# The down projection of the second feed-forward block: 16 of 22 contraction tiles by seven block products

## The chip, the cores and the metric

One Trainium2 chip, one of its cores. The metric is the device time of one execution in microseconds; a kernel's time is the median of its runs. A profile is one further execution with the hardware profiler, and the times of single instructions come from it. Engines are called TensorE (PE in the profile), VectorE (DVE), ScalarE (ACT), GpSimd (POOL) and SyncE (SP, which only issues transfers).

## The reference

One layer of a streaming encoder on x of 512 tokens by 1024 features, all in float32:

```
h = x + 0.5 * post1(SwiGLU_1(pre1(x)))          # SwiGLU: (silu(x @ w1) * (x @ w3)) @ w2
u = pre_mix(h)                                   # each pre/post: RMS norm with a gain
q, k, v, x_rnn, x_gate = split(u @ w_in)
y_a = (rg_lru(conv4(x_rnn)) * gelu(x_gate)) @ w_lru_out
y_b = sliding_window_attention(q, k, v) @ w_attn_out
merged = gate_a * y_a + gate_b * y_b             # gates: sigmoid(u @ w_gate + b_gate)
h = h + post_mix(merged @ w_o)
y = h + 0.5 * post2(SwiGLU_2(pre2(h)))
```

The hidden width of a feed-forward block is 2816. The change is in the last product, hidden (512 x 2816) @ w2 (2816 x 1024) of SwiGLU_2, named w2b in the kernel. What follows it is post2, the half and the addition of h.

## The kernel before

**Products in three terms.** A float32 operand is split into a high part in the matmul's number format (fp32r), copied by ScalarE, and a low part, the difference, taken by VectorE (`split2`, `split_to`). A product is three matmuls: high x high, high x low, low x high. In the down projections (`mm_tok`) the stationary operand is 128 hidden features by 128 tokens of the hidden activations and the moving one 128 features by 512 output columns of the weight. One contraction tile is 128 of the 2816 features; there are 22, and each has 4 token tiles x 2 column halves x 3 terms = 24 matmuls.

**The up projections.** After the first two tiles, w1 and w3 of both feed-forward blocks are computed in pairs of output tiles by a seven-product block scheme already (class `Pairs`): tokens, features and outputs are halved, block sums are made on GpSimd and VectorE, and seven block products of 128 x 256 outputs replace eight. Each pair is a job; `prep` makes a job's operands during the job before, `run` issues the products (`mm_s`) and the copies and sums that combine them out of PSUM. The results of FFN 2 are multiplied into hidden tiles, held in `Hidden`, which splits a tile when it is about to be used (`Hidden.to`).

**The down projection.** `tok_gemm` first runs over F = n - R tiles, all four token tiles for each, with eight accumulators in eight PSUM banks. The last R tiles (7 for w2b) are then run token tile by token tile, so that a token tile is complete, and its norm (`post_norm`) and store can run, while the next one is multiplied. `post_norm` squares a half on ScalarE (L292), multiplies by the gain on VectorE (L293), takes the reciprocal root (L256 to L264), and adds h (L304).

**What sets the order.** Each engine executes in the order in which the program is written. `get` names the next weight tile and with it issues loads (`dma_to`, SP's queue, in the list `order`) and splits some tiles ahead. `later` and `point` put small pieces of work between products: each `point` runs what is due. Tiles in SBUF come from a pool of 42 slots of 512 KB each; an instruction that writes a new tile waits for the last user of the slot's old one. PSUM has eight banks. Before the down projection ends the pair jobs: in the last job, `tail` is called twice, and each call splits one hidden tile and one weight tile of w2b.

**Residual.** h stays in four slots from the mixer's output GEMM (`wo`) to the end. In FFN 1 the corresponding tiles are written to memory (`spill`, `h_scr`) and loaded again later.

**Adding transfers.** In one other place a low part is made without VectorE (`split_dma`): ScalarE copies the high part and writes the negative of it (L160), and a transfer from memory in GpSimd's queue (L161) adds the raw weight onto it.

Of the kernel before, what the change touches and what calls it, by code (L numbers as in the profile page):

```python
# [13 lines left out]
ALU = mybir.AluOpType  # L14
# [37 lines left out]
def hybrid_layer(ctx: ExitStack, tc: tile.TileContext, a: dict, out: bass.AP):  # L52
# [48 lines left out]

    order = []

    def want(name, n):
        order.extend((name, i) for i in range(n))

    paired = set()

# [102 lines left out]
    def split2(hi, lo, src):  # L211

        act.activation(hi, src, AF.Copy)  # L213
        dve.tensor_tensor(out=lo, in0=src, in1=f32(hi), op=ALU.subtract)  # L214
# [18 lines left out]
        mm_feat(ps, w, **kw)  # L233
        return ps

    def mm_tok(acc, x, t, w, first, last, ns=(0, 1)):

        wh, wl = w
        c = slice(t * P, (t + 1) * P)
        for n in ns:  # L240
            s = slice(n * 512, (n + 1) * 512)
            pe.matmul(acc[n], x[:, 0, c], wh[:, s], start=first, stop=False)  # L242
            pe.matmul(acc[n], x[:, 0, c], wl[:, s], start=False, stop=False)  # L243
            pe.matmul(acc[n], x[:, 1, c], wh[:, s], start=False, stop=last)  # L244

# [38 lines left out]
    def post_norm(acc, t, gpost, scale, dst, after=None, last=False, eps=D * EPS, mid=None):  # L284

        ss = small(2, "ss")
        fg = slot([P, D], name="fg")
        junk = slot([P, D], name="junk")
        cs = [slice(n * 512, (n + 1) * 512) for n in range(2)]
        rs = Rstd2()  # L290
        for n, c in enumerate(cs):
            act.activation(junk[:, c], acc[n], AF.Square, accum_out=ss[:, n : n + 1])  # L292
            dve.scalar_tensor_tensor(out=fg[:, c], in0=acc[n], scalar=scale, in1=gpost[:, c], op0=ALU.mult, op1=ALU.mult)  # L293
            if n:
                rs.root(ss)
            else:
                rs.first(ss, eps)
        r = rs.value()
        if mid:
            mid()  # L300
        if last:
            cs = [slice(0, 512), slice(512, 768), slice(768, D)]
        for n, c in enumerate(cs):
            dve.scalar_tensor_tensor(out=dst[:, c], in0=fg[:, c], scalar=r, in1=h[t][:, c], op0=ALU.mult, op1=ALU.add)  # L304
            if after:
                after(n, c)
# [50 lines left out]
            act.activation(xf[half, t // 2][:, :, (t % 2) * P : (t % 2 + 1) * P], v, AF.Copy)  # L357


    def tok_gemm(nm, xs, n, R, gpost_name, scale, gpre_name, first, x_to=None, xf=None, spill=False, then=None, eps=None):  # L360

# [12 lines left out]
        pre = min(2, F)  # L374
        x_to = x_to or (lambda k: None)
        for k in range(pre):
            x_to(k + 1)
            w[k] = get(nm, k, ahead=pre - k + 1)
        if pre:
            for tt in ((0, 1), (2, 3)):  # L380
                for k in range(pre):
# [4 lines left out]
        for k in range(pre, F):  # L386
            x_to(k + 2)
            w[k] = get(nm, k, ahead=2 + (R - 2) * (k + 1) // F)
            for t in range(NT):
                mm_tok(accs(t), xs[k], t, w[k], k == 0, False)  # L390
                if t % 2:
                    point()
        point(True)
        for k in range(F, n):
            x_to(k + 1)
# [9 lines left out]
        for t in range(NT):  # L405
            for ns in ((0,), (1,)):
                for k in range(F, n):
                    mm_tok(accs(t), xs[k], t, w[k], k == 0, k == n - 1, ns)
            if not gpre_name:
                o = slot([P, D], name="o")  # L410

                def store(nn, c, t=t, o=o):
                    sp.dma_start(out=out[t * P : (t + 1) * P, c], in_=o[:, c])

                post_norm(acc[t], t, gpost, scale * NEWT, o, store, t == NT - 1)
# [55 lines left out]
        dma_to(st["split"] + 3)  # L471


    def silu_mul(ps1, ps3, t=None):

        t = t or slot([P, 2, SEQ], name="sw")
        act.activation(t[:, 0, :], ps1, AF.Silu)
        dve.tensor_tensor(out=t[:, 1, :], in0=ps3, in1=t[:, 0, :], op=ALU.mult)
        return t[:, 1, :]

    class Hidden:


        def __init__(self):
            self.f, self.t, self.done = [], {}, 0

        def to(self, n):
            while self.done < min(n, len(self.f)):
                assert self.f[self.done] is not None
                hT = slot([P, 2, SEQ], F32R, name="hT")  # L490
                split2(hT[:, 0, :], hT[:, 1, :], self.f[self.done])
                self.f[self.done] = None
                self.t[self.done] = hT
                self.done += 1

        def __getitem__(self, k):
            return self.t[k]

    QH = 4 * P

# [13 lines left out]
    class Pairs:  # L522
# [1 line left out]


        def __init__(self, names, f0, f1, X, hid=None, R=None):
            self.R = R
            self.jobs = [(nm, f) for f in range(f0, f1, 2) for nm in names]
            self.na, self.X, self.hid = names[0], X, hid
            self.k0 = order.index((self.na, f0))  # L530
            self.w, self.c1, self.ready = {}, {}, set()

        def raws(self, m):
            k = self.k0 + 2 * len(self.jobs)
            dma_to(min(self.k0 + 2 * m + 2, k) + max(0, m + 1 - len(self.jobs)))

        def prep(self, m, i, eng=None):
            if m >= len(self.jobs) or (m, i) in self.ready:
# [47 lines left out]
        def run(self, tail, hooks={}):  # L586
# [4 lines left out]
            for n, (nm, f) in enumerate(self.jobs):  # L591
# [47 lines left out]
                    c11()  # L639
                if not first:  # L640
                    c1 = self.c1[f]
                    dve.tensor_tensor(out=c1[:, 0, :], in0=c1[:, 0, :], in1=c[:, 0, :], op=ALU.mult)
                    dve.tensor_tensor(out=c1[:, 1, 256:], in0=c1[:, 1, 256:], in1=c[:, 1, 256:], op=ALU.mult)
                self.prep(n + 1, 4)
                self.prep(n + 2, 0)
                self.raws(n + 3)
# [1 line left out]
                def last(W=W, bu=bu, c=c, f=f, first=first):  # L648
                    mm_s(W.pop("a22"), X["t4"], bu, True)
                    if first and self.R is not None:  # L650
                        act.activation(c[:, 1, :256], bu, AF.Copy)
                        dve.tensor_tensor(out=c, in0=c, in1=self.R, op=ALU.mult)
                        return lambda: act.activation(c, c, AF.Silu)
                    if first:
                        act.activation(c[:, 1, :256], bu, AF.Silu)
                        act.activation(c[:, 0, :], c[:, 0, :], AF.Silu)
                        act.activation(c[:, 1, 256:], c[:, 1, 256:], AF.Silu)
                    else:
                        c1 = self.c1.pop(f)
                        dve.tensor_tensor(out=c1[:, 1, :256], in0=bu, in1=c1[:, 1, :256], op=ALU.mult)  # L660
                        self.hid.f += [c1[:, 0, :], c1[:, 1, :]]

            last()

# [174 lines left out]
    dma_to(NS + 2)  # L839

    hid, X1 = Hidden(), {}
    hid.f = [None] * NC1
    Rb = slot([P, 2, SEQ], name="Rb")
    pairs_a = Pairs(("w1a", "w3a"), NC1, FT, X1, hid, Rb)
    h_load([a["x"][t * P : (t + 1) * P, :] for t in range(NT)])
# [596 lines left out]
        mg.append(m)  # L1442


    hid, tn = Hidden(), []
# [15 lines left out]
    def operands():  # L1461
# [17 lines left out]
    hid.f.append(silu_mul(bs[0], bs[1]))  # L1479
    X2["t3"] = to_slots(tn[2])  # L1480
    hid.f.append(silu_mul(bs[2], bs[3]))
# [30 lines left out]

BY_POOL = {("wg", i) for i in range(2, 8)} | {("wk", 0), ("wk", 1)}
RF = 7
RO = 6

NC1 = 4
# [57 lines left out]
```

## Time and profile before

| | us |
|---|---|
| median of three runs (lowest, highest) | 1127.28 (1127.18, 1127.66) |
| span of the profiled execution | 1126.0 |
| up projections of FFN 2 by pairs | about 799 to 999 |
| down projection w2b on TensorE | 999.2 to 1119.1 |
| VectorE and ScalarE busy in 999.00 to 1119.30 | 49.74 and 37.62 |

The profile of an execution has several views. The page gives busy times and the costliest groups of instructions. A row of a group reads: line, engine, operation, output <- inputs, sizes, count | busy time, mean duration in ns of one | idle time before, and what ended it. A row of the timeline starts with start and duration in us, and in square brackets has the idle time before it and what ended that. A row of a stretch (from:to) gives its length, the busy time with the number of instructions of PE, PEld (weight loads of TensorE), DVE, ACT and POOL, then the granted TensorE clock as a share, the share of the DMA engines and GB/s. SPq and POOLq rows are issues of transfers.

### The profile page before, as it was taken

The page shows a single profiled execution, that of the slowest core. Times are in us where ns is not written, and L with a number is a line of the kernel's source. Part 1 is how long each engine was busy: PE and PEld are TensorE (multiplying, and loading weights), DVE is VectorE, ACT ScalarE, POOL GpSimd, SP SyncE. Part 2 cuts the span into 40 slices and gives each one's busy share as a digit, 9 for nine tenths or more (in the row PEclk, how much of TensorE's full clock was granted, in tenths as well). Part 3 has the DMA queues.
Part 4 walks back from the last instruction along what each step waited for, and adds up shares of the span by engine and source line. Part 5 has one row for each costly group of instructions (what it writes and reads, how often), then busy time and mean ns, then how long its engine had stood idle before and what let it go on. Part 6 is the DMA issues. An engine that isn't in the chain of part 4 may idle for free. (4 is left out here: it accounts for less than half of the span.)

```text
span 1126.0 us, 17883 instructions
## 1 busy us (share of the span) xinstructions
PE 1117.5 (99%) x6946; PEld 1008.3 (90%) x6946; DVE 828.6 (74%) x1225; ACT 620.2 (55%) x1107; POOL 367.0 (33%) x284
## 2 busy tenths in 40 slices
PE   9999999999999999999999999999999999999997
PEld 7899999988889877899888888889999999998886
DVE  5889989886436978887768867767897877975313
ACT  7755555574336678666655654456455555564211
POOL 0044444200101423242656663011765566700000
PEclk9999999999999999999999999999999999999999
DMA  9226563265214543156122336421333232265101
GB/s 346 100 82 149 132 133 113 76 224 166 97 62 153 149 117 101 38 173 239 59 92 75 131 112 225 179 103 40 111 108 102 92 113 86 88 201 170 37 20 56
DMA packets 40309, 136.52 MB, mean 121 GB/s; under 512 B 4880, under 2 KB 6800, under 8 KB 40224
## 3 DMA queue, kind: packets, MB, share of 16 engines
q1 hardware_dynamic: 36432, 123.28, 32.3%
q0 software_dynamic: 3504, 11.58, 5.2%
q8 instruction: 54, 0.88, 0.3%
q10 hardware_dynamic: 288, 0.52, 0.1%
q14 instruction: 31, 0.25, 0.1%
HBM read 121.74 MB, written 11.53 MB: 118 GB/s over the span
## 5 line engine op out<-in xcount | busy, mean ns | idle before, releaser
L517 PE MATMUL c<-uT,wlo 128*128 128x256 f32 x516 | 146.3, 283 | 0.0
L518 PE MATMUL c<-uT,whi 128*128 128x256 f32 x516 | 146.3, 283 | 0.0
L516 PE MATMUL c<-uT,whi 128*128 128x256 f32 x516 | 146.3, 283 | 0.0
L516 PE MATMUL c<-Xh,whi 128*128 128x256 f32 x504 | 143.0, 284 | 0.0
L517 PE MATMUL c<-Xh,wlo 128*128 128x256 f32 x504 | 143.0, 284 | 0.0
L242 PE MATMUL acc<-whi,hT 128*128 128x512 f32 x352 | 137.3, 390 | 0.0
L243 PE MATMUL acc<-wlo,hT 128*128 128x512 f32 x352 | 137.1, 390 | 0.0
L244 PE MATMUL acc<-whi,hT 128*128 128x512 f32 x352 | 137.1, 390 | 0.0
L224 PE MATMUL f<-uT,whi 128*128 128x512 f32 (+1 forms) x368 | 136.6, 371 | 0.0
L225 PE MATMUL f<-uT,wlo 128*128 128x512 f32 (+1 forms) x368 | 135.0, 367 | 0.0
L226 PE MATMUL f<-uT,whi 128*128 128x512 f32 (+1 forms) x368 | 135.0, 367 | 0.0
L214 DVE TENSOR_TENSOR wlo<-S,whi 128x1024 fp32r<-128x1024 f32 x86 | 125.2, 1456 | 7.4 <-ACT whi L213 3.5
L518 PE MATMUL c<-Xl,whi 128*128 128x256 f32 x456 | 129.3, 284 | 0.0
L213 ACT ACTIVATE whi<-S 128x1024 fp32r<-128x1024 f32 x86 | 88.3, 1054 | 23.1 <-DVE S L563 22.0
L516 PEld LDWEIGHTS c<-uT,whi 128*128 128x128 f32 x516 | 99.2, 192 | 0.2
L517 PEld LDWEIGHTS c<-uT,wlo 128*128 128x128 f32 x516 | 99.2, 192 | 0.2
L518 PEld LDWEIGHTS c<-uT,whi 128*128 128x128 f32 x516 | 99.2, 192 | 0.0
L516 PEld LDWEIGHTS c<-Xh,whi 128*128 128x128 f32 x504 | 96.9, 192 | 0.3 <-issue 0.3
L517 PEld LDWEIGHTS c<-Xh,wlo 128*128 128x128 f32 x504 | 96.9, 192 | 0.1
L518 PEld LDWEIGHTS c<-Xl,whi 128*128 128x128 f32 x456 | 87.7, 192 | 0.0
L224 PEld LDWEIGHTS f<-uT,whi 128*128 128x128 f32 x368 | 69.5, 189 | 12.5 <-issue 1.7
L226 PEld LDWEIGHTS f<-uT,whi 128*128 128x128 f32 x368 | 69.4, 189 | 11.4
(383 smaller groups left out, 2855.4 us busy)
## 6 DMA issues: line engine op xcount, KB each, us to landing
raw_w2a<-in_w2a_dram SPq DMA_DIRECT2D x22, 512.0 KB, 4.2
raw_w1b<-in_w1b_dram SPq DMA_DIRECT2D x22, 512.0 KB, 4.1
raw_w3b<-in_w3b_dram SPq DMA_DIRECT2D x22, 512.0 KB, 4.3
raw_w2b<-in_w2b_dram SPq DMA_DIRECT2D x22, 512.0 KB, 4.3
raw_w3a<-in_w3a_dram SPq DMA_DIRECT2D x21, 512.0 KB, 4.4
raw_w1a<-in_w1a_dram SPq DMA_DIRECT2D x20, 512.0 KB, 4.3
raw_wg<-in_wg_dram SPq DMA_DIRECT2D x16, 512.0 KB, 3.8
raw_xr<-in_xr_dram SPq DMA_DIRECT2D x8, 512.0 KB, 3.9
```

The costliest lines, as they stand in the source:

```text
L213: act.activation(hi, src, AF.Copy)
L214: dve.tensor_tensor(out=lo, in0=src, in1=f32(hi), op=ALU.subtract)
L224: pe.matmul(ps[:, c0:c1], wh[:, s], h_, start=k == 0 and c0 == 0, stop=False, skip_group_check=True)
L225: pe.matmul(ps[:, c0:c1], wl[:, s], h_, start=False, stop=False, skip_group_check=True)
L226: pe.matmul(ps[:, c0:c1], wh[:, s], l_, start=False, stop=k == KT - 1, skip_group_check=True)
L242: pe.matmul(acc[n], x[:, 0, c], wh[:, s], start=first, stop=False)
L243: pe.matmul(acc[n], x[:, 0, c], wl[:, s], start=False, stop=False)
L244: pe.matmul(acc[n], x[:, 1, c], wh[:, s], start=False, stop=last)
L516: pe.matmul(ps, wh[:, s], xh, start=first, stop=False, skip_group_check=True)
L517: pe.matmul(ps, wl[:, s], xh, start=False, stop=False, skip_group_check=True)
L518: pe.matmul(ps, wh[:, s], xl, start=False, stop=k == 3, skip_group_check=True)
```

## The change

The first 16 of w2b's 22 tiles are taken in four groups of four. In a group the hidden activations are four blocks (odd or even tiles, first or second half of the tokens) of 2 x 128 features by 256 tokens, the weight four blocks b11, b12, b21, b22 (first digit: first or second tile of each two; second digit: column half) of 2 x 128 features by 512 columns. The new class `Halves` forms seven products, m1 to m7, each over the four groups in turn: 28 units of 12 matmuls (2 contraction tiles x 2 token tiles x 3 terms), into three pairs of PSUM banks that are copied out or added on between products.

- All block sums (`T` of weights, `S` of hidden activations) are made on VectorE, in place in the raw blocks and in the hidden tiles.
- The low part of the weight operand in m1 and m2, which are blocks as loaded, is made by an adding transfer; in m3 the high part comes by a transfer too; in the other products VectorE makes the low part.
- Operands are prepared five units ahead (`LEAD`); units 0 to 3 in the two `tail` calls of the last pair job, instead of the first two tiles. Raw blocks are loaded from the last three pair jobs on (`LOAD_PAIRS`, `LOAD_AT`).
- The hidden tiles are written to slots of four tiles' common layout (`hEO`, `place`).
- Six tiles, not seven, are left for the part that runs token tile by token tile; they are loaded and split at fixed units (`RAW_TAIL`, `SPLIT_TAIL`). Their matmuls add onto banks left by the products; `post_norm` adds the copied-out parts on VectorE first (`part`).
- h is written to memory in the `wo` stage (`spill=True`) and loaded again at units 24 to 27 (`H_BACK`).

The diff, cut to its core:

```diff
-    want("w2b", FT)
+    want("w2b", FT, SF)
...
     def post_norm(..., mid=None, part=None):
+        if part:
+            acc = list(acc)
+            for n, o in enumerate(part):
+                if o is not None:
+                    dve.tensor_tensor(out=o, in0=acc[n], in1=o, op=ALU.add)
+                    acc[n] = o
...
     def tok_gemm(..., eps=None, pre=None):
+        if pre:
+            pre.run()
+            acc.update(pre.accs)
+        else:
...
-                    mm_tok(accs(t), xs[k], t, w[k], k == 0, k == n - 1, ns)
+                    mm_tok(accs(t), xs[k], t, w[k], k == F if pre and t > 1 and ns == (1,) else k == 0, k == n - 1, ns, bool(pre))
...
+    class Halves:
+        LOADS = tuple((b, i) for bs in (("b11", "b12"), ("b22", "b21")) for i in range(4) for b in bs)
+        NAMES = ("m1", "m5", "m2", "m6", "m7", "m3", "m4")
+        OPERANDS = {"m1": ("b11", 0, 0), "m2": ("b21", 1, 0), "m5": ("b12", 0, 1), "m6": ("b22", 0, 0), "m7": ("b11", 0, 1),
+                    "m3": ("b22", 1, 0), "m4": ("b21", 1, 1)}
+        BANK = {"m1": "bu", "m6": "bu", "m7": "bu", "m4": "bu", "m5": "bx", "m3": "bx", "m2": "bc"}
...
+        def sums(self, m, i):
+            if m == "m1":
+                self.T("b12", "b12", "b11", i)
+                self.S((0, 1), (0, 1), (1, 1), i, ALU.add)
+            elif m == "m5":
+                self.T("b22", "b22", "b12", i)
+                self.S((0, 0), (0, 1), (0, 0), i)
+                del self.raw["b12", i]
+            elif m == "m2":
+                self.T("b11", "b22", "b11", i)
+                self.S((1, 0), (1, 0), (0, 0), i)
+            elif m == "m6":
+                self.S((0, 1), (1, 1), (0, 0), i)
+            elif m == "m7":
+                self.T("b21", "b21", "b22", i)
+                del self.raw["b11", i], self.raw["b22", i]
...
+        def prep(self, n):
+            while self.ready < min(n, 28):
...
+                self.load(LOAD_AT(u))
...
+                if m == "m3":
+                    pool.dma_start(out=hi, in_=self.src(b, i))
+                    act.activation(lo, f32(hi), AF.Copy, scale=-1.0)
+                    pool.dma_start(out=lo, in_=self.src(b, i), accum_op=ALU.add)
+                else:
+                    src = self.raw[b, i]
+                    act.activation(hi, src, AF.Copy)
+                    if (m, i) in LO_DMA:
+                        act.activation(lo, src, AF.Copy, scale=-1.0)
+                        pool.dma_start(out=lo, in_=self.src(b, i), accum_op=ALU.add)
+                    else:
+                        dve.tensor_tensor(out=lo, in0=src, in1=f32(hi), op=ALU.subtract)
+                split2(xs[:, 0, :, :], xs[:, 1, :, :], self.x(i, odd, half))
+                self.ops[u] = hi, lo, xs
+                self.sums(m, i)
+
+        def unit(self, u):
...
+            for j in range(2):
+                for t, ps in enumerate(self.bank[key]):
+                    c = slice(t * P, (t + 1) * P)
+                    pe.matmul(ps, xs[:, 0, j, c], hi[:, j, :], start=start and j == 0, stop=False, skip_group_check=True)
+                    pe.matmul(ps, xs[:, 0, j, c], lo[:, j, :], start=False, stop=False, skip_group_check=True)
+                    pe.matmul(ps, xs[:, 1, j, c], hi[:, j, :], start=False, stop=u % 4 == 3, skip_group_check=True)
...
+        def out(self, m):
+            k, b = {"m1": ("q1", "bu"), "m5": ("q5", "bx"), "m6": ("u", "bu"), "m7": ("q5", "bu")}[m]
...
+                if m == "m7":
+                    dve.tensor_tensor(out=o, in0=ps, in1=o, op=ALU.add)
+                else:
+                    act.activation(o, ps, AF.Copy)
...
+        def run(self):
+            for u in range(28):
+                self.prep(u + LEAD)
+                for fn in self.hooks.get(u, ()):
+                    fn()
+                self.unit(u)
+                if u % 4 == 3 and self.NAMES[u // 4] in ("m1", "m5", "m6", "m7"):
+                    later(0, lambda m=self.NAMES[u // 4]: self.out(m), 0)
+                point()
...
-        [("w1b", 0), ("w3b", 0), ("w1b", 1), ("w3b", 1)], xf=xf, then=operands)
+        [("w1b", 0), ("w3b", 0), ("w1b", 1), ("w3b", 1)], xf=xf, spill=True, then=operands)
...
-    pairs_b.run(w2_ahead, late)
+    half = Halves("w2b", hid, hooks)
+    pairs_b.more = lambda n: half.load(LOAD_PAIRS[n])
+    pairs_b.run(lambda: half.prep(half.ready + AHEAD_PAIRS), late)
     X2 = pairs_b = None
-    tok_gemm("w2b", hid, FT, RF, "ffn2_post_g", 0.5, None, [], hid.to)
+    tok_gemm("w2b", hid, FT, FT - SF, "ffn2_post_g", 0.5, None, [], hid.to, pre=half)
...
+SF = 16
+LEAD = 5
+LO_DMA = {(m, i) for m in ("m1", "m2") for i in range(4)}
+LOAD_PAIRS = (0, 4, 6, 8)
+AHEAD_PAIRS = 2
+RAW_TAIL = (14, 16, 18, 20, 22, 24)
+SPLIT_TAIL = (16, 18, 20, 22, 24, 26)
+H_BACK = (24, 25, 26, 27)
+
+def LOAD_AT(u):
+    return min(16, 9 + u)
```

More of the change, by code (lines that the diff above doesn't have):

```diff
@@ L102, in hybrid_layer, with want @@
     order = []
-    def want(name, n):
-        order.extend((name, i) for i in range(n))
+    def want(name, n, first=0):
+        order.extend((name, i) for i in range(first, n))
     paired = set()
@@ L234, in unit, with mm_tok @@
         return ps
-    def mm_tok(acc, x, t, w, first, last, ns=(0, 1)):
+    def mm_tok(acc, x, t, w, first, last, ns=(0, 1), skip=False):
         wh, wl = w
@@ L282, in bcast, with post_norm @@
         return t
-    def post_norm(acc, t, gpost, scale, dst, after=None, last=False, eps=D * EPS, mid=None):
+    def post_norm(acc, t, gpost, scale, dst, after=None, last=False, eps=D * EPS, mid=None, part=None):
         ss = small(2, "ss")
@@ L372, in accs @@
             return acc[t]
-        pre = min(2, F)
         x_to = x_to or (lambda k: None)
-        for k in range(pre):
-            x_to(k + 1)
-            w[k] = get(nm, k, ahead=pre - k + 1)
         if pre:
+            pre.run()
+            acc.update(pre.accs)
+        else:
+            both = min(2, F)
+            for k in range(both):
+                x_to(k + 1)
+                w[k] = get(nm, k, ahead=both - k + 1)
             for tt in ((0, 1), (2, 3)):
-                for k in range(pre):
+                for k in range(both):
                     for t in tt:
@@ L385, in tok_gemm @@
                             point()
[L386 to L392, printed above, removed]
+            for k in range(both, F):
+                x_to(k + 2)
+                w[k] = get(nm, k, ahead=2 + (R - 2) * (k + 1) // F)
+                for t in range(NT):
+                    mm_tok(accs(t), xs[k], t, w[k], k == 0, False)
+                    if t % 2:
+                        point()
         point(True)
@@ L413, in store @@
                     sp.dma_start(out=out[t * P : (t + 1) * P, c], in_=o[:, c])
-                post_norm(acc[t], t, gpost, scale * NEWT, o, store, t == NT - 1)
+                post_norm(acc[t], t, gpost, scale * NEWT, o, store, t == NT - 1, part=pre and pre.part(t))
                 continue
@@ L533, in raws @@
         def raws(self, m):
-            k = self.k0 + 2 * len(self.jobs)
-            dma_to(min(self.k0 + 2 * m + 2, k) + max(0, m + 1 - len(self.jobs)))
+            k, more = self.k0 + 2 * len(self.jobs), max(0, m + 1 - len(self.jobs))
+            dma_to(min(self.k0 + 2 * m + 2, k) + (0 if self.more else more))
+            if self.more and more:
+                self.more(more)
         def prep(self, m, i, eng=None):
@@ L1442, in mg_out @@
         mg.append(m)
[L1445 removed]
+    hid, tn = Hidden(SF), []
     X2 = {"b11": uview(0, 0), "b21": uview(1, 0), "b22": uview(1, 1)}
```

113 lines of the change are left out of this document (92 added, 21 removed).

## The prediction

> **What bounds the kernel now.** I read the page first, then busy time by stretches, then the chain of waits in order of time, then the groups by form, and last the timelines of VectorE, ScalarE and GpSimd around the stage that is edited.
>
> ```profile
> span 1126.0 us, 17883 instructions
> PE 1117.5 (99%) x6946; PEld 1008.3 (90%) x6946; DVE 828.6 (74%) x1225; ACT 620.2 (55%) x1107; POOL 367.0 (33%) x284
> 990.00:1000.00 10.00, 10.00 (x83) 9.87 (x82) 4.84 (x7) 6.89 (x12) 0.00 (x0) 1.00 0.81 268
> 999.00:1119.30 120.30, 120.10 (x532) 99.24 (x530) 49.74 (x71) 37.62 (x59) 0.59 (x1) 1.00 0.25 84
> 1119.30:1126.00 6.70, 0.00 (x0) 0.00 (x0) 2.84 (x7) 0.82 (x3) 0.00 (x0) 0.65 0.21 78
> 999.39 0.23 PE acc L242
> 1118.87 0.24 PE acc L244
> L242 PE MATMUL acc<-whi,hT 128*128 128x512 f32 x176 | 68.6, 390 | 0.0
> ```
>
> TensorE is busy 99% of the span, and in the last GEMM (999.00 to 1119.30, the third row of stretches being what comes after it) it is busy throughout, at full granted clock, while VectorE is busy for 49.74 us and ScalarE for 37.62. The chain runs on TensorE from 999.39 to 1118.87 and then 7 us through ScalarE, VectorE and the store. So the stage is bound by the number of matmuls. Each of its three lines has 176 matmuls, 528 in all. Their 390 ns are latency, not pace: by the chain, 527 steps take 1118.87 - 999.39 = 119.48 us, 0.2267 us each.
>
> **The change, removed.** Sixteen of the 22 tiles had 16 x 24 = 384 matmuls. Seven products, in four groups, over two contraction halves, two token tiles and three high/low terms, are 7 x 4 x 12 = 336, with the same 128x128 against 128x512. That is 48 x 0.2267 = 10.9 us less. One unit (12 matmuls) lasts 2.72 us, the 28 units 76.2 us, the six tiles left 144 x 0.2267 = 32.6 us.
>
> **VectorE and ScalarE, added.** Prices, with GpSimd idle and (second row) beside its sums:
>
> ```profile
> L179 DVE TENSOR_TENSOR wlo<-raw_w2b,whi 128x1024 fp32r<-128x1024 f32 x22 | 26.5, 1221 | 9.5 <-ACT whi L178 6.6 <-issue 1.5 <-PE acc L243 1.3
> L214 DVE TENSOR_TENSOR wlo<-S,whi 128x1024 fp32r<-128x1024 f32 x22 | 36.4, 1653 | 2.2 <-ACT whi L213 2.1
> L214 DVE TENSOR_TENSOR w<-raw_w3b,w 128x512 fp32r<-128x512 f32 x6 | 5.2, 864 | 0.1
> L887 DVE TENSOR_TENSOR T<-xg,xg 128x1024 f32<-128x1024 f32 x2 | 2.4, 1219 | 0.0
> 1007.05 0.68 DVE L214 TENSOR_TENSOR hT<-cc,hT 128x512 fp32r<-128x512 f32 x1
> 1007.66 1.21 DVE L179 TENSOR_TENSOR wlo<-raw_w2b,whi 128x1024 fp32r<-128x1024 f32 x1
> 1008.79 0.68 DVE L214 TENSOR_TENSOR hT<-cc,hT 128x512 fp32r<-128x512 f32 x1
> 997.35 2.94 ACT L178 ACTIVATE whi<-raw_w2b 128x1024 fp32r<-128x1024 f32 x3
> 1000.20 1.14 ACT L213 ACTIVATE hT<-cc 128x512 fp32r<-128x512 f32 x2
> ```
>
> Start to start on VectorE, a 1024-wide subtraction costs 1.13 us and a 512-wide one 0.61. On ScalarE three 1024-wide copies in 2.94 and two 512-wide in 1.14 give 0.95 and 0.52. Per unit on VectorE: m1 and m2 (low part by transfer; x low part, a weight sum, a hidden sum) 0.61 + 1.13 + 0.61 = 2.35; m5 the same and its low part, 3.48; m6 1.13 + 0.61 + 0.61 = 2.35; m7 1.13 + 0.61 + 1.13 = 2.87; m3 0.61; m4 1.74. Four times their sum is 63.0 us. The tail's splits, 6 x 1.74 = 10.4, and m7's two sums out of PSUM bring 75 us, against 76.2 us of TensorE. VectorE is cover with hardly any slack, so I walk its queue below. ScalarE: 2.42 a unit in m1 and m2, 1.47 in the others, with copies out of banks and tail some 60 us: cover.
>
> **The end.** For the last token tile a sum of bank and stored part stands on VectorE ahead of both halves:
>
> ```profile
> 1118.71 0.39 PE L244 MATMUL acc<-whi,hT 128*128 128x512 f32 x1
> 1119.14 0.60 ACT L292 ACTIVATE junk<-acc 128x512 f32<-128x512 f32 x1 [4.07 <-PE acc L244]
> 1119.86 0.69 DVE L293 SCALAR_TENSOR_TENSOR fg<-acc,bc_ffn_post_g 128x512 f32<-128x512 f32 x1 [4.01 <-ACT junk L292]
> 1120.46 0.20 DVE L260 TENSOR_SCALAR v<-ss,b 128x1 f32<-128x1 f32 x1
> 1121.41 1.54 DVE L304 SCALAR_TENSOR_TENSOR o<-fg,r,h 128x512 f32<-128x512 f32 x3
> ```
>
> ScalarE's square starts 0.43 us after the last matmul does. VectorE will do from that point: the sum (0.61), the first half's product, which used to be early (0.61), the small add (0.07), the second half's product (0.61). Then v is at +2.33 us instead of 1120.46 - 1118.71 = 1.75: **0.6 us**. If the product still waits for the square, 0.8. For the earlier token tiles the 4.08 us of a half hide it.
>
> **The start.** The last pair job now prepares units 0 to 3 where it prepared two tiles:
>
> ```profile
> 974.95 65.79 SPq L146 DMA_DIRECT2D raw_w2b<-in_w2b_dram  x22
> 993.67 0.38 ACT L613 ACTIVATE ct<-c 128x256 f32<-128x256 f32 x1 [0.17 <-PE c L518]
> 993.95 0.62 ACT L213 ACTIVATE hT<-sw 128x512 fp32r<-128x512 f32 x1
> 996.55 0.38 ACT L635 ACTIVATE ct<-c 128x256 f32<-128x256 f32 x1 [1.03 <-PE c L518]
> 997.79 0.28 PE L516 MATMUL c<-uT,w 128*128 128x256 f32 x1
> 999.23 0.40 PE L242 MATMUL acc<-whi,hT 128*128 128x512 f32 x1
> ```
>
> Behind the copy at 993.67 ScalarE now has two units, 2 x 2.42 us, ahead of the L635 copy: it moves from 996.55 to 998.8. The last product of the pair job adds onto that bank and waits for the copy's end, 999.2: it starts 1.46 us later than 997.79, and unit 0 starts at 1000.7 instead of 999.23. Queued behind units 0 and 1 are only these copies and units 2 and 3; VectorE's sums there free banks that nobody needs yet.
>
> The low part of a raw block comes by an adding transfer from GpSimd's queue. The nearest rows are six such transfers between 379 and 403 us:
>
> ```profile
> 381.60 1.05 ACT L160 ACTIVATE wlo<-raw_wg 128x1024 fp32r<-128x1024 f32 x1
> 382.95 0.89 POOL L161 DMA_DIRECT2D wlo<-in_wg_dram x1 [1.86 <-ACT wlo L160]
> L161 POOL DMA_DIRECT2D wlo<-xf x4: 861/870/978, 380.1 to 395.0; - x4
> wlo<-in_wg_dram POOLq DMA_DIRECT2D x2, 512.0 KB, 7.2
> DMA to landing us min/median/max: 4.5/6.3/9.7
> q0 software_dynamic: 851, 3.12, 70.2%
> 379.00:403.00 24.00, 24.00 (x111) 19.38 (x110) 18.50 (x27) 18.69 (x23) 8.36 (x9) 1.00 0.94 217
> ```
>
> Landing took 4.5 to 9.7 us, 7.2 for the two from weights in memory. I take 7.2: same source, and transfers as busy (0.94) as they will be here with 16 raw loads and four adds together. Unit 0's negative copy ends at 993.95 + 0.95 + 1.05 = 995.95; the transfer is issued 0.3 later (382.95 after a copy that ended at 382.65) and lands at 1003.45; unit 0's second matmul waits for it and the unit ends at 1005.95. Landings of units 1 to 3 (1005.9, 1008.6, 1011.0; one unit of ScalarE apart and the L635 copy between) then come just in time: m1 ends at 1014.1 and m5 at 1025.0. VectorE starts unit 1 when ScalarE has copied its x, 993.95 + 2 x 2.42 = 998.8, and is done with it at 1001.3; two sums of the pair job (0.33 each) and units 2 and 3 bring it to 1006.65, the pair job's four last sums to 1008.3; unit 7's parts ready after 3 x 3.48 + 1.74 at 1020.5, wanted at 1022.3; no wait. Without stalls m5 would end at 999.23 + 8 x 2.72 = 1021.0: **4.0 us** lost. With landings in 4.5 us the VectorE walk limits m5 and 2.1 are lost; with 9.7, 6.5.
>
> ScalarE copies m1 out of its banks behind m1's last matmul, and only then takes unit 8: 1014.1 + 0.43 (as the square at the end) + 1.1 (two copies) + 2.0 (high part and negative copy) + 0.3 + 7.2 = 1025.1 for its landing, wanted at 1025.2. No loss; at 9.7 another 2.4. Capacity: 3.12 MB in 70.2% of 24 us are 2.81 us of all 16 engines for one adding transfer; 268 GB/s at a share of 0.81 make 1.58 us for a plain 512 KB. Twelve adds and 30 plain transfers (16 raw blocks, 4 direct high parts, 6 tail tiles, 4 reloads of h) are 81 us out of the 110 from 975, where the raw loads of w2b begin now, to the tail: late, but not the bound.
>
> VectorE to m7: 1008.3 + 4 x (3.48 + 2.35 + 2.35 + 2.87) = 1052.5, unit 19's parts at 1051.4, wanted at 1055.4. m3 then leaves VectorE nearly idle, so tail splits and m4 are covered. m3's high part comes by transfer too, but GpSimd has nothing before it since unit 11.
>
> [...] GpSimd spent 0.86 to 0.98 us on each issue while VectorE was busy for 18.50 of 24 us. [...]
>
> **m7 behind m6 in one bank.** m7 adds onto the banks that ScalarE is to copy out after m6. A copy starts 0.43 us after the last matmul on its bank and takes 0.6 (the square's rows); that bank's last matmul lies three before the unit's end, 0.7 us. So 0.3 to 0.6: I take **0.5 us**; below nothing is excluded, since the wait is new.
>
> **The wo stage.** Spilling h puts four stores into SP's queue ahead of the two loads of w3b; each store waits for its h.
>
> ```profile
> 772.85 0.80 SPq L146 DMA_DIRECT2D raw_w3b<-in_w3b_dram  x2
> 776.02 1.41 DVE L304 SCALAR_TENSOR_TENSOR h<-fg,r,h 128x512 f32<-128x512 f32 x2
> 786.99 2.27 POOL L567 TENSOR_TENSOR S<-raw_w3b 128x512 f32<-128x512 f32 x1
> raw_w3b<-in_w3b_dram SPq DMA_DIRECT2D x22, 512.0 KB, 4.3
> ```
>
> The last h is written at 777.4, the loads go at about 778 instead of 772.85 and land by 783.3; GpSimd takes them at 786.99. Nothing, with 3.7 us of cover; without it the first sums of job 1 would be late by what is missing. Writing the hidden tiles to other slots moves no instruction: nothing.
>
> **Sum.** -10.9 + 4.0 + 0.5 + 0.6 = -5.8 us on the profiled span of 1126.0, which stands 1.28 below the median of 1127.28; I give the difference to the median: **1121.5 us**. With the ends 2.1 and 6.5 for the start, 1119.6 to 1124.0.
>
> **The rivals.** *Nothing waits* (1117.0): landings are early, slots let preparation run further ahead, only the end's 0.6 is paid: -10.3. For it speaks that ScalarE and VectorE idle at times in this stage now; against it the L635 copy, which no early landing moves.
>
> *Transfers land late* (1126.4): at 9.7 us the start costs 6.5 and unit 8 another 2.4: -10.9 + 6.5 + 2.4 + 0.5 + 0.6 = -0.9. For it speaks the 0.94 share. TensorE would then idle some 5 us in one piece, and the stretch after 1119.30 shows the granted clock fall to 0.65 when TensorE stops. [...]
>
> *VectorE becomes the bound, and the kernel slower* (1136.0). If its subtractions run as they do beside GpSimd's sums, 1653 instead of 1221 ns and 864 instead of 680, then up to unit 19 it has 28 x 0.43 + 36 x 0.18 = 18.5 us more; less the 4.0 of cover there 14.5 are lost: +8.7. It decides from 9.8 us more on, a 1024-wide mean of about 1.45 us. Against it: GpSimd only issues transfers here, and beside such issues no slow subtraction is seen. For it: cover of 1.8 us at unit 7 means that any wait of VectorE for ScalarE, a slot or a raw block is paid almost whole.
>
> **How the numbers follow.** Forecast 0.50, nothing waits 0.14, late landings 0.14, VectorE bound 0.22. What can be told from no change is 0.2%, 2.25 us. Faster: 0.50 + 0.14 = 0.64. Late landings lie within 0.2%, but for 0.02 with landings beyond 10 us: same 0.12, slower 0.22 + 0.02 = 0.24. The range goes from 1117.0 to 1132.0: it leaves out the worse two thirds of the VectorE case (0.15) and a little of the other end (0.05).
>
> **What would show it.** 336 matmuls of the new lines with TensorE waiting at some 1000 and 1001 to 1003.5 us, the second time for a transfer; m5 with VectorE busy without a break; a short wait at the first unit of m7; unit 19 not waiting for VectorE; the last store's start 0.6 us later after the last matmul. Wrong would make it: 1024-wide subtractions over 1.45 us, landings beyond 10 us, waits in m3 for its two transfers in a row, or stalls in the pair jobs because raw blocks hold their slots.

## The result, and the profile after

The changed kernel takes 1145.75 us (median of four runs, 1145.03 to 1146.36) where the one before takes 1127.47 (1127.18 to 1127.94). The ratio is 1.0163 with a 95% interval of 1.0148 to 1.0177: slower by 18.3 us. The forecast was 5.8 us faster, with a range that ended at 1132.0. The profiled execution of the changed kernel has a span of 1144.6 us, 18.6 more than that of before.

The line numbers below are those of the changed kernel: L609 to L611 are the three terms of a product unit (`Halves.unit`), L584 to L586 the three steps of m3's weight operand (high part by a transfer, negative copy on ScalarE, adding transfer), L592 the adding transfer of m1 and m2.

The head of its page, and what TensorE waits for between 995 and 1140 us (total, times, longest):

```profile
span 1144.6 us, 17962 instructions
PE 1116.8 (98%) x6898; PEld 1004.4 (88%) x6898; DVE 876.7 (77%) x1277; ACT 648.5 (57%) x1145; POOL 383.5 (34%) x300
...
PE hw L610 <- DMA wlo<-in_w2b_dram: 18.0, 4, 5.2
PE c L654 <- ACT ct L775: 1.3, 1, 1.3
```

The 48 matmuls are gone (6946 to 6898), and VectorE has 48 us more to do. But TensorE, which did not wait in this stage before, now waits four times for an adding transfer, 18.0 us in all, and once for the copy that stands behind the new work on ScalarE. For VectorE it doesn't wait. The same stage in stretches of 10 us, in the columns explained above (length, PE, PEld, DVE, ACT, POOL, granted clock, DMA share, GB/s):

```profile
1000.00:1010.00 10.00, 4.77 (x18) 3.69 (x17) 9.97 (x17) 6.65 (x9) 2.37 (x2) 0.83 1.07 220
1010.00:1020.00 10.00, 10.00 (x45) 8.26 (x45) 10.00 (x12) 5.32 (x8) 0.00 (x0) 1.00 0.56 153
1060.00:1070.00 10.00, 5.87 (x27) 4.54 (x26) 0.69 (x1) 1.58 (x2) 1.95 (x2) 1.00 0.79 190
1070.00:1080.00 10.00, 5.85 (x16) 4.09 (x15) 2.52 (x3) 3.04 (x4) 1.95 (x2) 0.69 0.62 159
1080.00:1090.00 10.00, 5.52 (x14) 3.83 (x13) 7.74 (x10) 9.35 (x13) 1.19 (x1) 0.67 0.62 162
1090.00:1100.00 10.00, 10.00 (x37) 8.04 (x36) 8.04 (x10) 4.08 (x6) 0.58 (x1) 0.79 0.41 150
```

There are two holes: one at the start (first row) and one from 1060 to 1100, which is m3. In the second, TensorE is busy a little over half of the time while VectorE and ScalarE have almost nothing to do from 1060 to 1070 and no engine is full before 1080; the granted clock then falls as well (0.69 and 0.67 in the two stretches from 1070 to 1090). The waits in TensorE's timeline:

```profile
998.95 0.38 PE L654 MATMUL c<-uT,w 128*128 128x256 f32 x1 [1.25 <-ACT ct L775]
...
1000.49 0.39 PE L609 MATMUL hw<-whi,hx 128*128 128x512 f32 x1
1006.11 0.79 PE L610 MATMUL hw<-wlo,hx 128*128 128x512 f32 x1 [5.23 <-DMA wlo<-in_w2b_dram]
...
1069.36 0.50 PE L610 MATMUL hw<-wlo,uT 128*128 128x512 f32 x1 [4.13 <-DMA wlo<-in_w2b_dram]
...
1078.11 0.80 PE L610 MATMUL hw<-wlo,uT 128*128 128x512 f32 x1 [4.15 <-DMA wlo<-in_w2b_dram]
...
1088.09 0.80 PE L610 MATMUL hw<-wlo,uT 128*128 128x512 f32 x1 [4.48 <-DMA wlo<-in_w2b_dram]
...
1089.11 0.63 PE L609 MATMUL hw<-whi,uT 128*128 128x512 f32 x1
1089.54 0.63 PE L610 MATMUL hw<-wlo,uT 128*128 128x512 f32 x1
```

Each is the second matmul of a unit, the first that needs the low part: of unit 0 (1006.11) and of units 21, 22 and 23, the last three of m3. After these four waits (4.1 to 5.2 us) the matmuls step by 0.43 us (1089.11 to 1089.54) instead of 0.2267.

These rows close the account. The step from each matmul to the next, less 0.2267, is over by 6.8 us in unit 0 (5.4 around the wait, the rest slow steps), by 0.3 at the first unit of m7, and by 20.4 in m3 (13.7 around its three waits, 6.7 in slow steps after them, the last of which fall in m4). Unit 0 begins 1.26 later than the old first matmul (1000.49 against 999.23), 10.9 us of matmuls are gone, and the end is 0.4 longer. So 1.3 + 6.8 + 0.3 + 20.4 + 0.4 - 10.9 = 18.3, against 18.6 measured between the two spans; the 0.3 left over lies in steps that are a few hundredths of a us too long. The start costs 8.1, and m3, costed at nothing, 20.4.

Why m3 waits is seen in GpSimd's queue, here its timeline in m3, and below it five rows of ScalarE's (L623 copies m6 out of its banks):

```profile
1043.20 0.75 POOL L584 DMA_DIRECT2D whi<-in_w2b_dram  x1 [13.52 <-PE hw L611]
1052.93 1.19 POOL L586 DMA_DIRECT2D wlo<-in_w2b_dram  x1 [8.99 <-ACT wlo L585]
1053.68 1.21 POOL L584 DMA_DIRECT2D whi<-in_w2b_dram  x1
1063.78 1.19 POOL L586 DMA_DIRECT2D wlo<-in_w2b_dram  x1 [8.89 <-ACT wlo L585]
1064.52 1.21 POOL L584 DMA_DIRECT2D whi<-in_w2b_dram  x1
1072.56 1.19 POOL L586 DMA_DIRECT2D wlo<-in_w2b_dram  x1 [6.82 <-ACT wlo L585]
1073.29 1.21 POOL L584 DMA_DIRECT2D whi<-in_w2b_dram  x1
1082.01 1.19 POOL L586 DMA_DIRECT2D wlo<-in_w2b_dram  x1 [7.50 <-ACT wlo L585]
```

```profile
1050.41 1.28 ACT L623 ACTIVATE hc<-hw 128x512 f32<-128x512 f32 x2 [8.73 <-PE hw L611]
1051.58 1.05 ACT L585 ACTIVATE wlo<-whi 128x1024 fp32r<-128x1024 f32 x1
...
1062.42 1.06 ACT L585 ACTIVATE wlo<-whi 128x1024 fp32r<-128x1024 f32 x1 [7.81 <-DMA whi<-in_w2b_dram]
...
1071.20 1.06 ACT L585 ACTIVATE wlo<-whi 128x1024 fp32r<-128x1024 f32 x1 [7.20 <-DMA whi<-in_w2b_dram]
...
1080.65 1.06 ACT L585 ACTIVATE wlo<-whi 128x1024 fp32r<-128x1024 f32 x1 [6.41 <-DMA whi<-in_w2b_dram]
```

GpSimd issues in the order of the program: high part of unit 20, adding transfer of unit 20, high part of unit 21, and so on. The adding transfer waits for ScalarE's negative copy (every L586 row names it), and from unit 21 on that copy waits for the high part to land (the last three L585 rows). So the high part of a unit, which depends on nothing but a slot, is issued 0.75 us after the adding transfer of the unit before, and that one only when its own high part has landed. A unit takes a landing, a copy and an issue, one after the other: 1052.93 to 1063.78 to 1072.56 to 1082.01, 9.7 us on average, where TensorE needs one every 2.72. That units are prepared five ahead buys a head start and nothing more.

Two things make it worse. The landing itself is longer in this order: the first high part, with nothing ahead of it, landed 4.2 us after its issue, the next three, issued right behind an adding transfer, 8.7, 6.6 and 7.3 us after theirs, each 1.4 to 2.5 us after that adding transfer had landed. And part of the head start is lost on ScalarE: unit 20's negative copy (1051.58) doesn't wait for its high part, which landed at about 1047.4, but stands behind the copies of m6, which wait for m6's last matmul.

### The profile page after: what moved, and what is told of

The parts are those of the page before. It is cut to its first block, busy times and chain, and to the rows that moved or that the text cites. A ratio compares the mean times of both kernels' runs of the same rounds, so it can differ in the third digit from the quotient of the medians.

```text
span 1144.6 us, 17962 instructions
## 1 busy us (share of the span) xinstructions
PE 1116.8 (98%) x6898; PEld 1004.4 (88%) x6898; DVE 876.7 (77%) x1277; ACT 648.5 (57%) x1145; POOL 383.5 (34%) x300
## 5 line engine op out<-in xcount | busy, mean ns | idle before, releaser
L214 DVE TENSOR_TENSOR wlo<-S,whi 128x1024 fp32r<-128x1024 f32 x86 | 120.1, 1397 | 6.5 <-POOL OL L1529 3.1
L225 PEld LDWEIGHTS f<-uT,wlo 128*128 128x128 f32 x368 | 69.4, 189 | 10.7
L1477 POOL TENSOR_SCALAR P<-P,d 128x256 f32<-128x256 f32 (+1 forms) x64 | 62.6, 993 | 45.5 <-DVE d L1475 25.7
L242 PE MATMUL acc<-whi,hT 128*128 128x512 f32 x188 | 73.3, 390 | 0.0
```

Of the source, the lines that this page charges most:

```text
L225: pe.matmul(ps[:, c0:c1], wl[:, s], h_, start=False, stop=False, skip_group_check=True)
L1477: pool.tensor_scalar(out=pt[:, x, b0:256], in0=pt[:, x, b0:256], scalar1=d[:, x : x + 1], scalar2=None, op0=ALU.mult)
```

## The experiments

Theory Q (queue): m3's transfers stand in a row in GpSimd's queue, and that is the greater part of the loss. Theory S (start): unit 0's adding transfer is issued too late and lands too slowly. Theory C (clock): a good part of the loss is the lower clock after the waits. Theory V (VectorE): VectorE has no slack, and bounds the stage as soon as anything delays it. The "after" in what follows is the changed kernel.

**m3's four high parts ahead of its adding transfers.** The same transfers in another order.

```diff
+                if m == "m3" and i == 0:
+                    self.his = [slot([P, 2, 512], F32R, name="whi") for _ in range(4)]
+                    for n_, t_ in enumerate(self.his):
+                        pool.dma_start(out=t_, in_=self.src(b, n_))
...
-                    pool.dma_start(out=hi, in_=self.src(b, i))
```

> The changed kernel with one edit: the four transfers of m3's high parts are issued together when unit 20 is prepared, ahead of m3's adding transfers in GpSimd's queue. Queue theory (in m3 each high-part transfer stands in GpSimd's queue behind the adding transfer of the unit before, which waits for ScalarE's copy, which waits for the high part): the three waits of TensorE in m3, 4.1 to 4.5 us each, and most of the half-clock stretches behind them go; some 18 to 21 us less than the changed kernel, about 1125 us. Slow-transfer theory (landings of 6 to 9 us are what the load on the DMA engines makes of them): the waits stay, under 6 us less. VectorE theory (it is the bound): under 3 us less.

Measured: 1128.17 us (1126.75 to 1131.31, ten runs), 17.6 less than after; to before 1.0004 (0.9995 to 1.0014). GpSimd's timeline in m3 of this kernel, and what TensorE still waits for:

```profile
1044.48 0.74 POOL L581 DMA_DIRECT2D whi<-in_w2b_dram  x1 [13.52 <-PE hw L615]
1046.97 2.15 POOL L581 DMA_DIRECT2D whi<-in_w2b_dram  x3 [1.75 <-PE hw L615]
1054.22 1.21 POOL L590 DMA_DIRECT2D wlo<-in_w2b_dram  x1 [5.09 <-ACT wlo L589]
1057.16 1.19 POOL L590 DMA_DIRECT2D wlo<-in_w2b_dram  x1 [1.73 <-ACT wlo L589]
1058.62 1.19 POOL L590 DMA_DIRECT2D wlo<-in_w2b_dram  x1 [0.27 <-ACT wlo L589]
1061.55 1.18 POOL L590 DMA_DIRECT2D wlo<-in_w2b_dram  x1 [1.75 <-ACT wlo L589]
```

```profile
PE hw L614 <- DMA wlo<-in_w2b_dram: 5.1, 1, 5.1
PE c L658 <- ACT ct L779: 1.3, 1, 1.3
```

With the same number of transfers and bytes the four adding transfers now go out within 7.3 us (1054.22 to 1061.55) instead of 29.1 (1052.93 to 1082.01), and no wait is left in m3. These adding transfers land in 6.3 to 10.4 us, later after their issue than those of m3 in after (5.5 to 8.1), and none of ScalarE's copies waits for a high part any more (three did in after, 21.4 us in all). Unit 20's negative copy stands behind m6's copies here too (its adding transfer goes out at 1054.22, later than in after), and that costs nothing. It was the order in the queue. The gain is a little short of the 18 to 21 us expected; unit 0 loses 8.3 us here (with its slow steps), not 6.8. What is left of the stage's waits is the start, and with it the kernel is even with before.

**m3 without GpSimd.** Its four blocks are loaded once more by SP's queue into new slots and split by ScalarE and VectorE.

```diff
-                    pool.dma_start(out=hi, in_=self.src(b, i))
-                    act.activation(lo, f32(hi), AF.Copy, scale=-1.0)
-                    pool.dma_start(out=lo, in_=self.src(b, i), accum_op=ALU.add)
-                else:
-                    src = self.raw[b, i]
+                    if i == 0:
+                        self.again = [slot([P, 2, 512], name="again") for _ in range(4)]
+                        for n_, t_ in enumerate(self.again):
+                            sp.dma_start(out=t_, in_=self.src(b, n_))
+                if True:
+                    src = self.again[i] if m == "m3" else self.raw[b, i]
```

> The changed kernel without GpSimd's transfers in m3: the four b22 blocks are loaded a second time through SP's queue and split by ScalarE and VectorE as in m4. Queue theory: as for the run with the high parts first, 18 to 22 us less than the changed kernel, 1124 to 1128 us. VectorE theory: 4 x 1.13 us more of VectorE's work make it no better than the changed kernel by more than 3 us. Slow-transfer theory: 18 to 22 us less too, since the adding transfers of m3 are gone.

Measured: 1126.22 us (1124.88 to 1127.44, ten runs), 19.5 less than after; to before 0.9988 (0.9978 to 0.9998). The start's two waits remain (4.3 and 1.3 us), and again none in m3. VectorE has 4.5 us more here (four low parts at 1.13), and it doesn't show. Two different ways around the row of transfers give 17.6 and 19.5 of the 20.4 us that the account puts on m3.

**m1's low parts on VectorE.** The four adding transfers at the start are left out, m3 is as in after.

```diff
-LO_DMA = {(m, i) for m in ("m1", "m2") for i in range(4)}
+LO_DMA = {(m, i) for m in ("m2",) for i in range(4)}
```

> The changed kernel with m1's four low parts made by VectorE instead of adding transfers. Start theory (unit 0 waits 5.2 us for its adding transfer, and the last pair product 1.3 us for a copy behind two units of ScalarE): both waits and the half clock behind the first go, 8 us; VectorE has 4.5 us more to do before m5 and gives back 3 to 5 us: 1141 to 1143 us. VectorE theory: slower than the changed kernel by up to 4 us, 1146 to 1150.

Measured: 1141.76 us (1141.11 to 1142.93, four runs), 4.0 less than after; to before 1.0122 (1.0107 to 1.0137). The waits of TensorE:

```profile
PE hw L610 <- DMA wlo<-in_w2b_dram: 12.5, 3, 4.7
PE hw L610 <- DVE wlo L594: 1.8, 1, 1.8
```

The waits at the start, for the transfer and for the copy, are gone, the three of m3 (12.5 us) stay, and VectorE shows up once, with 1.8 us. That one line is not the whole price. Counted in steps over 0.2267 us as above, the profiled runs are 5.3 us apart: the start gives back 8.7 (unit 0 loses nothing and begins at 998.63 instead of 1000.49), m3 loses 1.5 less, and 4.5 us more on VectorE cost 5.0, namely 2.0 around the listed wait (unit 4), 1.8 in the slow steps behind it and 1.2 in units 3, 5 and 7, which show no wait. VectorE has next to no slack there, as the start theory expected (3 to 5 us given back).

**Filler matmuls in the waits.** 22, 17, 17 and 18 matmuls into an unused bank ahead of the four that wait, so that TensorE stays busy; the transfers are those of after.

```diff
+                    if u in FILL and j == t == 0:
+                        spare = bank("fill")
+                        for n_ in range(FILL[u]):
+                            pe.matmul(spare, xs[:, 0, j, c], hi[:, j, :], start=True, stop=True)
...
+FILL = {0: 22, 21: 17, 22: 17, 23: 18}
```

> The changed kernel with matmuls into a spare bank, whose result is not used, ahead of the four matmuls of units 0, 21, 22 and 23 that wait for a transfer: 22, 17, 17 and 18 of them, about as long as the waits. It shows what the fallen clock costs beside the waits. If the clock behind a wait costs time of its own: the half-clock stretches after 1006 and after 1088 us go, 1.4 and 2.9 us, and 3 to 5 us less than the changed kernel, 1141 to 1143; those behind units 21 and 22 gain nothing, since the next unit waits for GpSimd's queue in any case. If only the waits count: within 1 us of 1145.75.

Measured: 1144.07 us (1141.83 to 1145.20, four runs), 1.7 less than after; the ratios to before are 1.0139 (1.0124 to 1.0154) and 1.0163 (1.0148 to 1.0177) and their intervals overlap. That lies between the two expectations. TensorE's longest wait in the stage is 2.6 us here and the granted clock is 1.00 in every stretch of it, so the clock does fall because TensorE waits. What that is worth by itself the run leaves between nothing and some 4 us. The account gives the same size: the slow steps after unit 0 (1.4 us) and after unit 23 (3.0) are paid, those after units 21 and 22 only shorten the next wait for a transfer. The clock is a consequence that adds at most some 4 us, not the cause.

**The start, earlier.** m3 as in the second experiment; unit 0 is prepared in the last but one pair job, unit 1 at the beginning of the last, units 2 and 3 in its two `tail` calls; fewer raw blocks are loaded with units 0 and 1 (`LOAD_AT`).

```diff
+    late[len(pairs_b.jobs) - 2, 3] = [lambda: half.prep(1)]
+    late[len(pairs_b.jobs) - 1, 1] = [lambda: half.prep(2)]
...
-    pairs_b.run(lambda: half.prep(half.ready + AHEAD_PAIRS), late)
+    pairs_b.run(lambda: half.prep(half.ready + 1), late)
...
-    return min(16, 9 + u)
+    return min(16, 9 + u) if u > 1 else 2 * u + 2
```

> The run with m3's blocks reloaded, and unit 0 prepared in the last pair job but one, unit 1 at the beginning of the last one, units 2 and 3 where units 0 to 3 were. Start theory (the start costs 1.3 us of waiting for the L775 copy, 4.3 to 5.2 for unit 0's adding transfer, which is issued too late, and some 1.5 of half clock behind it): all three go, 7 to 8 us less than the run with m3 reloaded, 1117 to 1119.5 us, faster than the kernel before. VectorE theory (without these waits VectorE, busy without a break from 996 to 1052 us there, sets the pace): only 2 to 4 us less, 1122 to 1124.

Measured: 1121.58 us (1120.81 to 1122.13, five runs); to before 0.9950 (0.9938 to 0.9963), faster than before and than after. Its span, the wait for transfers that is left, and the first stretch:

```profile
span 1119.7 us, 17942 instructions
...
PE hw L611 <- DMA wlo<-in_w2b_dram: 2.3, 2, 1.3
...
1000.00:1010.00 10.00, 8.66 (x37) 6.33 (x35) 9.97 (x15) 5.67 (x8) 0.75 (x1) 1.00 1.09 272
```

It came out between what the start theory (1117 to 1119.5) and the VectorE theory (1122 to 1124) expected, close to the second, though the only waits listed in this stage are for transfers. 4.6 us of the start are back, compared with the second experiment. Units 2 and 3 still wait 1.3 and 1.0 us: their adding transfers, issued at 996.94 and 999.57, land about 10 and 11.4 us later, in a stretch where the DMA share is 1.09. The granted clock stays at 1.00.

**No adding transfers at all,** and, as its counterpart, **only m2's**. Both have m3 from the second experiment; VectorE makes the low parts that the transfers made.

```diff
-LO_DMA = {(m, i) for m in ("m1", "m2") for i in range(4)}
+LO_DMA = set()
```

> The run with m3's blocks reloaded, and all low parts made by VectorE, no adding transfer at all. VectorE has 8 x 1.13 = 9.0 us more to do up to m2's end. If VectorE's cover is as small as the prediction had it (1.8 us at unit 7, 4.0 at unit 19): the start's waits (7 to 8 us) go and as much is lost again to waits for VectorE in m5 and m2, 1125 to 1128 us. If VectorE is far from the bound: 1118 to 1120.

> The run with m3's blocks reloaded, and m1's low parts by VectorE, m2's by adding transfers. The waits at the start go, VectorE has 4.5 us more and TensorE waits for it in m5: as much less as m1 on VectorE gave the changed kernel, 4 us: 1121 to 1123. If VectorE is far from the bound: 1118 to 1120.

Measured: 1126.68 us (1126.25 to 1127.63, ten runs; to before 0.9996, 0.9987 to 1.0005) with none, and 1122.62 (1122.49 to 1123.30, four runs; to before 0.9959, 0.9944 to 0.9974) with those of m2. Taking m1's away gains 3.6 us over the second experiment, because nothing at the start waits for a landing any more. Taking m2's away too puts 4.5 us more on VectorE and costs 4.1. In the kernel without any, TensorE's one listed wait for VectorE is 1.8 us; but units 5 to 12 each take 0.7 to 0.8 us too long, 8.9 us with units 3 and 4, and the chain of waits in order of time runs along VectorE; four of its pieces:

```profile
1002.31 1.14 DVE wlo L595
1004.04 1.14 DVE raw_w2b L545
...
1031.83 1.13 DVE wlo L595
...
1035.31 1.13 DVE wlo L595
```

With 9 us more VectorE is the bound from about 1000 to 1040 us. So the adding transfers of m2 do what they are there for: they keep VectorE from becoming the bound. Those of m1, issued where the changed kernel issues them, cost more than they save; issued earlier, as in the fifth experiment (1121.58 us, 1120.81 to 1122.13), they do no worse than VectorE (1122.62).

## Why the prediction was wrong

**The step that failed** is the one on m3: "m3 then leaves VectorE nearly idle, so tail splits and m4 are covered. m3's high part comes by transfer too, but GpSimd has nothing before it since unit 11." GpSimd was free for m3's first unit, as the sentence says, and the idleness of the engines is true as well (0.69 us of VectorE in 1060 to 1070). But it asked who stands in the queue before m3, not what m3's own eight transfers do to each other. By the prediction's own numbers a unit would have been a landing, 1.05 us of copy, 0.3 and another issue: with landings of 4.5 to 9.7, some 7 to 12 us a unit against 2.72. They were all on the page; the queue was not walked. Measured: 20.4 us by the account, 17.6 and 19.5 by the two experiments. "Waits in m3 for its two transfers in a row" stood among what would make the prediction wrong, without a price or a chance.

**The start: mechanism right, size off.** The copy that moved behind ScalarE's new work made the last product of the pair job late (998.95 instead of 997.79; 1.16 us measured, 1.46 forecast), and unit 0's adding transfer was issued when the forecast had it:

```profile
996.25 9.82 DMA wlo<-in_w2b_dram
```

The landing, taken as 7.2, was 9.8, at the upper end of the quoted six; the sum then gives 6.5, as the prediction said for 9.7, and the slow clock after the wait 1.4 more. Measured 8.1 instead of 4.0. The term was mis-sized in its landing, which was taken from two transfers at a DMA share of 0.94; the share here is 0.83 in 990 to 1000 and 1.07 in the 10 us after it. m2's four landed in 5.9 to 6.4 us, with no transfer of SP's beside them. That SP's loads made unit 0's longer fits, but isn't shown. The remark that the granted clock falls when TensorE stops was right in kind: here it was at half (0.50 in 1007 to 1008, 1071 to 1072, 1079 to 1080 and 1089 to 1090) after waits of 4.1 to 5.2 us, and stayed at 1.00 behind waits of 1.0 and 1.3 us (the fifth experiment). But it also fell behind waits of 1.8 us in the third experiment (steps of 0.43 us from 1013.51 to 1016.07) and in the seventh (0.91 over 1012 to 1030, the longest matmul 0.63 us), and stayed at 1.00 behind one as long in the sixth. So the length of a single wait doesn't settle it here.

**What came as forecast.** The 48 matmuls at 0.2267 us. VectorE's prices and its queue:

```profile
1006.35 0.41 DVE L764 TENSOR_TENSOR cc<-c,ct 128x256 f32<-128x256 f32 x1
...
1008.08 1.21 DVE L594 TENSOR_TENSOR wlo<-raw_w2b,whi 128x1024 fp32r<-128x1024 f32 x1
1009.21 0.68 DVE L214 TENSOR_TENSOR uT<-hEO,uT 128x512 fp32r<-128x512 f32 x1
1009.81 1.21 DVE L545 TENSOR_TENSOR raw_w2b<-raw_w2b,raw_w2b 128x1024 f32<-128x1024 f32 x1
```

Units 2 and 3 were to be done at 1006.65 and unit 4 to begin at 1008.3; it was 1006.35 and 1008.08, at 1.13 and 0.60 from start to start. That VectorE has hardly any slack was right too: once nothing waits at the start, 4.5 us more cost 5.0 and 5.1 (the third and the seventh experiment, slow steps included), 9 us more 8.9 (the sixth). These are not the cover of the changed kernel itself, where the waits at the start give VectorE time. Unit 8 did not wait. The first unit of m7 lost 0.3 (forecast 0.5). The wo stage cost nothing: the copy that stood at 993.67 starts at 993.42. The end:

```profile
1136.91 0.39 PE L244 MATMUL acc<-whi,hT 128*128 128x512 f32 x1
1137.33 0.69 DVE L294 TENSOR_TENSOR hc<-acc,hc 128x512 f32<-128x512 f32 x1 [4.00 <-PE acc L244]
...
1139.20 0.20 DVE L260 TENSOR_SCALAR v<-ss,b 128x1 f32<-128x1 f32 x1
```

From the last matmul to v it takes 2.29 us, forecast 2.33, before 1.75.

**The rivals.** "Nothing waits" fell. "Transfers land late" happened at the start, though not at unit 8, and didn't bring the total by itself. "VectorE becomes the bound" had most of the chance for a slower kernel and did not happen in the changed kernel; it does where its low parts are all put on VectorE. The kernel was slower by a mechanism that none of the rivals priced. The forecast of 1121.5 is almost what the fifth experiment measures (1121.58), but that agreement proves little: that kernel has no start loss of 4.0, and other terms instead.

**What stays open.** Even with m3 and the start mended some 4.6 us lie between 1121.58 and the 1117.0 of "nothing waits"; the trace accounts for 4.0 of them: unit 0 begins 0.45 late (a product of the pair job waits 0.6 for VectorE), units 2 and 3 are 2.9 too long, other steps 0.5, the end 0.1 longer than forecast. The other 0.6 is how much further the median lies from the profiled span than in the run before. And the price of the clock alone is known only to within some 4 us.

## What to carry to other kernels

A transfer that needed nothing still waited here for everything ahead of it in its engine's queue (m3's high parts went out 0.75 us behind adding transfers that came 9.7 us apart; issuing them first gave 17.6 us): where a step issues two dependent transfers on one queue, write down the queue for two units in a row, and issue the independent ones of all units first. Engines that are idle are no evidence that a stage is covered (from 1060 to 1070 VectorE was busy for 0.69 us and TensorE for 5.87); this stage, whose operands each pass through landing, copy and landing again, was set by that latency (9.7 us a unit against 2.72) with units prepared five ahead, until the passes overlapped. Where a low part can be made by an engine or by a transfer, take the transfer where the engine's slack is gone and the landing has notice enough (adding transfers took 5.4 to 11.4 us to land in the changed kernel and the experiments; m2's saved 4.1 us), and the engine where the operand is wanted at once (m1's on VectorE gained 3.6).

## What the runs showed of the hardware beyond that

The granted clock fell within the changed kernel with waits of 4.1 to 5.2 us (and in two of the experiments with one of 1.8 us, as said above): 0.67 to 0.83 over 10 us, steps of 0.43 instead of 0.2267 us for 3 to 6 us after the matmul restarts. After the wait that ended at 1069.36 TensorE still ran at full speed for a microsecond and only then slowed (1.00 in 1069 to 1070, 0.70 and 0.50 in the two microseconds after); at the other three the clock had fallen before the wait ended (0.78 in 1005 to 1006, 0.61 in 1077 to 1078, 0.73 in 1087 to 1088).

Issuing an adding transfer took GpSimd 1.19 us here, against 0.86 to 0.98 for the six of before, though both carry 512 KB, and the time from issue to landing was long and uneven. The rows below are those of m3's high parts, of its adding transfers, and of the adding transfers of m1 and m2, all of the changed kernel:

```profile
DMA to landing us min/median/max: 4.2/6.9/8.7
DMA to landing us min/median/max: 5.5/5.8/8.1
DMA to landing us min/median/max: 5.9/8.1/10.4
```

The two sets of four adding transfers of m1 and m2 in the changed kernel, issued at about the same pace, landed differently: m1's in 9.8 to 10.4 us, while SP's queue moved 1.79 MB beside them (996 to 1014 us), m2's in 5.9 to 6.4, while it moved nothing (1021 to 1035 us). But these stretches differ in other things too, and one of m3's landed in 5.5 us beside 0.43 MB of SP's (1063.7 to 1069.4 us), so it isn't shown that SP's transfers make the difference.
